# Last weight columns copied within DRAM during the scan, and the first closing loads moved into the unit in front

## The chip, the cores and the metric

The kernel runs on one NeuronCore of a Trainium2 chip. The metric is the device time of one execution in microseconds: the median of several runs. A separate execution was profiled; every row below comes from it. The engines are TensorE (PE, with its weight loads as PEld), VectorE (DVE), ScalarE (ACT), GpSimd (POOL) and SyncE (SP), which computes nothing and issues nearly all DMAs. POOL issues the DMAs that add into DRAM.

## The reference, cut to what matters

One decoder layer on 1024 tokens with 2048 channels, in float32, and a closing norm:

```python
hn = rmsnorm(h, norm_gain)
proj = hn @ w_in                       # pool input | pool gate | SSM input | SSM gate
ya = pool_mixer(pool_in, w_pool, pool_scale) * silu(pool_gate)
yb = ssm_mixer(ssm_in, ..., w_glu) * silu(ssm_gate)    # a complex-diagonal scan, then GELU and GLU
h = h + concatenate([ya, yb]) @ w_out
h = h + (p @ w_ple) * sigmoid(h @ w_ple_gate)
return rmsnorm(h, final_gain)
```

The change touches the last product, `h @ w_ple_gate`, in its last 512 of 2048 output columns, and what is loaded for it.

## The kernel before

Every float32 operand of a large product is split into a high and a low part that PE can multiply at full rate: ACT casts the high part (L213, L203, L401, L1415, L1430), DVE subtracts to get the low part (all on the helper line L102), and three matmuls (high-high, high-low, low-high) replace one. The program is a hand-written list of `steps`, each with its matmuls, a list `pre` of what is issued in front of them and `post` of what follows. `emit(s)` goes through them in order; it also splits the weights of the next steps and issues loads of the next weight chunks (buffers `raw`, three of them) ahead of time. Nothing reorders the instructions afterwards: each engine and SP's queue work in the order in which they are written. An instruction that waits holds up all that stands behind it on its engine.

The stretches that matter here:

- **Input projection and scan.** Blocks of `hn @ w_in` (L257) fill PE. Beside them a generator issues the state-space work piece by piece. One piece of it (`ss_v`) loads pairs `vb` and `vu` (sixteen groups, 0 to 15, each 256 KB and 256 KB) and multiplies them on PE (L881) into `aux`, in between the projection's matmuls.
- **Fourteen units.** Eight for `w_out`, six for the first 1536 columns of `w_ple_gate`; each unit forms the seven products of a Strassen-like scheme in fourteen steps (L235). The operands are 28 slots of a pool of 32 (`s_p`), called `cb`; a product's four slots are used for the last time in the last unit of a half, and come free there product by product. A step's result is added by DVE to `zs`; where it is the last part, ACT takes the sigmoid, DVE multiplies by `ze`, and POOL adds the tile into `z_d` in DRAM (L1323). Later steps go on adding into a bank whose intermediate value was read before.
- **Closing blocks.** The last 512 columns are done by token blocks (`tb` 0 to 7, 128 tokens each), four steps of twelve matmuls a block (L247), with the weights `wl` resident (16 tiles, one for each 128 rows) and the rows of `h` as the stationary side. In front of a step PE turns a tile `zn` (or the rows of `h` for the group g = 3) by four transposes into `bk` (L1454); the turned rows are normed and written out.

For block 0 all this must be there when the last unit (first step `s_l`) ends: the sixteen `wl` tiles, loaded by `wl_load` into the three `raw` buffers and split by `wl_split` into slots (L1409, L1415), four tiles of `h` (`h_load`, `h_split`, L1423, L1430), the tiles `zn`, and `fg`, the closing gain broadcast to all partitions (L1400, L1404).

Of the kernel before, what the change touches and what calls it, by code (L numbers as in the profile page):

```python
# [8 lines left out]
F32 = mybir.dt.float32  # L9
# [3 lines left out]
ALU = mybir.AluOpType  # L13
# [3 lines left out]
P = 128  # L17
L = 1024
HT = 512
D = 2048  # L20
# [19 lines left out]
def hybrid_trunk(ctx: ExitStack, tc: tile.TileContext, x, p, norm_gain, w_in, w_pool, pool_scale,  # L40
# [3 lines left out]
    sp = nc.sync  # L44
    dve = nc.vector
    act = nc.scalar
# [4 lines left out]
    p = p[0, 0]  # L51
    out = out[0]
# [5 lines left out]
    w_ple_gate = w_ple_gate[0].rearrange("(k p) c -> p k c", p=P)  # L58
# [4 lines left out]
    r_p = ctx.enter_context(tc.tile_pool(name="r_p", bufs=3))  # L63
# [16 lines left out]
    e_d = dr.tile([3 * HT, L], F32, name="e_d")  # L80
    en_d = dr.tile([L, HT], F32, name="en_d")
    ps_d = dr.tile([3 * HT, L], F32, name="ps_d")
    z_d = dr.tile([3 * HT, L], F32, name="z_d")
    gq_d = dr.tile([W, L], F32, name="gq_d")
    B_d = dr.tile([P, G, P], F32, name="B_d")
# [3 lines left out]
    def st(dt=F32, shape=(P, HT), name="st"):  # L89
        return st_p.tile(list(shape), dt, tag="st", name=name)  # L90

    def slot(name):
        return s_p.tile([P, 2, HT], F32R, tag="S", name=name)
# [4 lines left out]
    def f(ap):  # L98
        return ap.bitcast(F32)

    def tt(eng, o, a, b, op):
        eng.tensor_tensor(out=o, in0=a, in1=b, op=op)  # L102
# [1009 lines left out]
    def in_block(mb, halves=(0, 1)):  # L1112
        block(in_cols(mb), ALLK, halves, hn_key, ("pi", mb), v_post(mb))
        if 1 in halves:
            steps[-1]["post"].append(lambda: bg.append(pool_win(mb // 2, mb % 2)))
# [10 lines left out]
    in_block(6)  # L1126
    in_block(7)
    i_g = len(steps)
    in_block(4)
    pool_mm(3)  # L1130
    in_block(5)
# [273 lines left out]
                         in_=final_gain[L + i * GW:L + (i + 1) * GW].partition_broadcast(P))  # L1405

    def wl_load(k):
        fin["wl", k] = r_p.tile([P, 4, P], F32, tag="raw", name="raw").rearrange("p a c -> p (a c)")
        sp.dma_start(out=fin["wl", k], in_=w_ple_gate[:, k, 3 * GW:])  # L1409

    def wl_split(k):
        raw = fin.pop(("wl", k))
        sl = slot("wl")
        acts["wl", k] = sl[:, 0], sl[:, 1]
        act.copy(out=sl[:, 0], in_=raw)  # L1415
        tt(dve, sl[:, 1], raw, f(sl[:, 0]), ALU.subtract)

    def rows4(src, g, tb):
        return src[4 * g * P:4 * (g + 1) * P, tok(tb)].rearrange("(k q) t -> q k t", q=P)
# [11 lines left out]
        tt(dve, sl[:, 1], f(sl[:, 1]), f(sl[:, 0]), ALU.subtract)  # L1431

    def zn_load(tb, g):
        fin["z", tb, g] = st(name="zn")
        sp.dma_start(out=fin["z", tb, g].rearrange("p (k t) -> p k t", k=4),
                     in_=rows4(xT_d if g == 3 else z_d, g, tb))

# [78 lines left out]
                                     (lambda i=part.start // 256: last_part(i)))  # L1516
    s_l = units[-1][1]
    for k in range(KD):
        at = s_l + 2 + 3 * k // 4
        steps[at]["pre"].append(lambda k=k: wl_load(k))  # L1520
        steps[at + 2]["pre"].append(lambda k=k: wl_split(k))
    steps[i_t[0] - 2]["pre"].append(fg_load)
    for tb in range(NB):
        for g in range(4):
            at = s_l + 10 + g if tb == 0 else i_t[0] + g - 2 if tb == 1 else i_t[tb - 2] + g
            steps[at]["pre"].append(lambda tb=tb, g=g: h_load(tb, g))
            at = max(at + 3, i_t[tb - 1] + g) if tb else s_l + 13
            steps[at]["pre"].append(lambda tb=tb, g=g: h_split(tb, g))
            if tb == 0:
                at = i_t[0] + {3: 1, 0: 2, 1: 3, 2: 4}[g]  # L1530
            else:
                at = i_t[tb] + g + (tb == 1)
                if (tb, g) == (1, 3):
                    at -= 1
            steps[at - 3]["pre"].append(lambda tb=tb, g=g: zn_load(tb, g))
            steps[at]["pre"].append(lambda tb=tb, g=g: z_turn(tb, g))
        steps[i_t[tb]]["pre"].append(lambda tb=tb: en_load(tb))
        if tb < NB - 1:
            steps[i_t[tb + 1] + 2]["pre"].append(lambda tb=tb: final(tb))
# [70 lines left out]
```

## Time and profile before

| | |
|---|---|
| median of the runs | 1704.83 us (1703.92 to 1708.3) |
| the profiled execution | 1705.38 us, of which the span of instructions 1703.3 us |
| PE busy | 97% of the span |
| DVE, ACT, POOL busy | 66%, 42%, 9% |
| mean DMA rate | 198 GB/s |

The span is what the profiler saw from the first to the last instruction; the profiled execution has another 2.1 us around it. Busy shares are averages over stages with different limits. A row of a timeline gives start, length, engine, line, operation, tiles, count, and in brackets the idle time of the engine in front of it with what ended it. SPq rows are SP issuing a DMA: the time is that of the issue, not of the transfer. The granted clock of PE is a share of 2.4 GHz.

### The profile page before, as it was taken

What the parts mean: (1) busy time and instruction counts of PE and PEld (TensorE: products, weight loads), DVE (VectorE), ACT (ScalarE), POOL (GpSimd) and SP (SyncE); (2) the same over time, 40 slices, a digit from 0 to 9 for tenths busy, and PEclk for the clock granted to TensorE, in tenths of its full rate; (3) what the DMA queues carried; (4) which work ended last, traced back from release to release, by engine and by line L of the source; (5) the groups of instructions that cost most, each with busy time, mean ns of one, the idle gap of its engine ahead of it and who ended that gap; (6) DMA issues with size and microseconds to landing.
All of it is one profiled execution on the core that took longest, in us unless ns stands there. A gap on an engine that the chain in (4) does not pass through costs nothing.

```text
span 1703.3 us, 22940 instructions
## 1 busy us (share of the span) xinstructions
PE 1655.8 (97%) x7622; PEld 1369.0 (80%) x7622; DVE 1115.7 (66%) x2148; ACT 718.2 (42%) x1511; POOL 160.2 (9%) x267
## 2 busy tenths in 40 slices
PE   8999999999999999999999999999998899999797
PEld 7888887888888888888778877888886788787686
DVE  5763699468786645656646787658456756877554
ACT  6652255352113642333643354336333534434453
POOL 0067000000000210000000001111111100021000
PEclk9999999999999999999999999999999899999899
DMA  8872444462233753667955668868679957888995
GB/s 260 251 191 73 117 133 135 155 186 75 68 118 117 230 173 103 193 194 240 328 210 173 210 250 244 229 167 241 159 194 275 302 208 277 273 212 212 298 268 159
DMA packets 332104, 336.41 MB, mean 198 GB/s; under 512 B 56025, under 2 KB 225010, under 8 KB 330994
## 3 DMA queue, kind: packets, MB, share of 16 engines
q1 hardware_dynamic: 319314, 311.88, 57.1%
q0 software_dynamic: 12672, 23.07, 8.6%
q8 instruction: 60, 0.98, 0.2%
q14 instruction: 58, 0.48, 0.1%
HBM read 222.15 MB, written 119.01 MB: 200 GB/s over the span
## 4 chain that ended last, share of the span: by engine, by line
PE 47%; DMA 6%; DVE 3%; issue 2%; ACT 1%; SPq 0%; ACTq 0%; POOLq 0%; POOL 0%; DVEq 0%
PE mm L235 23%; PE aux L235 9%; PE mm L257 9%; PE mm L247 5%; DMA cb<-cm_d 1%; DMA cm_d<-cq 1%; DMA raw<-in_w_ple_gate_dram 1%; PE bk L1454 1%; DVE cb L102 1%; DMA e_d<-et 1%; DMA cb<-ya_d 1%; DMA zn<-xT_d 1%; DVE w L102 1%; DVE zs L102 0%; DMA cb<-xT_d 0%
## 5 line engine op out<-in xcount | busy, mean ns | idle before, releaser
L257 PE MATMUL mm<-hn,w 128*128 128x512 f32 x3072 | 722.2, 393 | 1.8 <-DVE w L102 1.2
L257 PEld LDWEIGHTS mm<-hn,w 128*128 128x128 f32 x3072 | 572.2, 188 | 119.7 <-DVE w L102 1.7
L235 PE MATMUL mm<-cb,w 128*128 128x512 f32 x2160 | 500.8, 391 | 8.6 <-ACT w L203 3.1
L235 PEld LDWEIGHTS mm<-cb,w 128*128 128x128 f32 x2160 | 405.4, 188 | 98.2 <-DVE w L102 5.1
L213 ACT CAST w<-raw 128x256 fp32r<-128x256 f32 x324 | 128.2, 407 | 279.4 <-PE mm L257 219.1
L102 DVE TENSOR_TENSOR w<-raw,w 128x256 fp32r<-128x256 f32 (+1 forms) x328 | 141.0, 441 | 121.4 <-ACT w L213 113.3
L102 DVE TENSOR_TENSOR w<-wq,w 128x512 fp32r<-128x512 f32 x216 | 148.3, 686 | 104.0 <-ACT w L203 103.7
L235 PE MATMUL aux<-cb,w 128*128 128x512 f32 x864 | 205.5, 393 | 7.7 <-ACT w L203 7.7
L235 PEld LDWEIGHTS aux<-cb,w 128*128 128x128 f32 x864 | 163.0, 189 | 44.4 <-ACT w L203 9.3
L203 ACT CAST w<-wq 128x512 fp32r<-128x512 f32 x216 | 133.6, 620 | 134.3 <-PE mm L235 54.8
L1286 POOL DMA_DIRECT2D xT_d<-ot x64 | 55.4, 866 | 670.3 <-DVE ot L102 634.7
L102 DVE TENSOR_TENSOR cb<-cb 128x512 fp32r<-128x512 f32 x140 | 91.6, 685 | 32.8 <-ACT cb L401 32.3
L247 PE MATMUL mm<-wl,h 128*128 128x512 f32 (+1 forms) x432 | 100.9, 386 | 5.7 <-ACT h L1430 5.7
L401 ACT CAST cb<-cb 128x512 fp32r<-128x512 f32 x140 | 82.3, 621 | 40.8 <-DMA cb<-xT_d 13.7
L247 PEld LDWEIGHTS mm<-wl,h 128*128 128x128 f32 x432 | 75.7, 196 | 19.2 <-ACT h L1430 6.1
L102 POOL TENSOR_TENSOR ytm<-yt,mask 128x512 f32<-128x512 f32 x16 | 20.0, 1250 | 441.5 <-DMA yl<-L_d 310.7
L1292 ACT COPY ot<-mm 128x512 f32<-128x512 f32 x48 | 28.2, 587 | 75.7 <-PE mm L235 73.3
L102 DVE TENSOR_TENSOR wq<-wq 128x1024 f32<-128x1024 f32 x36 | 43.8, 1217 | 0.0
L499 ACT ACTIVATE gs<-mm 128x512 f32<-128x512 f32 x32 | 18.9, 598 | 58.3 <-DVE mm L102 57.0
L1323 POOL DMA_DIRECT2D z_d<-zs x24 | 20.7, 863 | 230.0 <-DVE zs L102 230.0
L891 DVE COPY V<-aux 64x128 f32<-64x128 f32 x64 | 24.6, 384 | 25.2 <-ACT V L893 24.8
L102 DVE TENSOR_TENSOR w<-t,w 128x512 fp32r<-128x512 f32 x36 | 24.5, 685 | 19.2 <-ACT w L203 19.2
(209 smaller groups left out, 1558.1 us busy)
## 6 DMA issues: line engine op xcount, KB each, us to landing
raw<-in_w_in_dram SPq DMA_DIRECT2D x136, 256.0 KB, 2.9
cb<-cm_d SPq DMA_DIRECT2D x80, 256.0 KB, 5.2
wq<-in_w_out_dram SPq DMA_DIRECT2D x16, 1024.0 KB, 9.0
xT_d<-ot POOLq DMA_DIRECT2D x64, 256.0 KB, 6.4
cm_d<-cq SPq DMA_DIRECT2D x48, 256.0 KB, 3.9
wq<-in_w_ple_gate_dram SPq DMA_DIRECT2D x12, 1024.0 KB, 9.1
xT_d<-xt SPq DMA_DIRECT2D x32, 256.0 KB, 4.2
wq<-in_w_glu_dram SPq DMA_DIRECT2D x16, 512.0 KB, 6.9
```

What stands on the lines that cost most here:

```text
L102: eng.tensor_tensor(out=o, in0=a, in1=b, op=op)
L203: act.copy(out=w[0], in_=src)
L213: act.copy(out=w[:, 0], in_=raw)
L235: pe.matmul(out=banks[key], lhsT=w[wi][:, kp], rhs=a[:, ai], start=bool(new) and n == 0, stop=n == 11, skip_group_check=True)
L247: pe.matmul(out=banks[key][:, part], lhsT=a[:, ai, cols], rhs=b[:, part], start=start and j == 0, stop=stop and j == 2)
L257: pe.matmul(out=banks[key], lhsT=w[:, wi, i], rhs=a[:, ai], start=start and i == 0 and j == 0, stop=stop and i == 1 and j == 2)
L401: act.copy(out=sl[:, 0], in_=f(sl[:, 1]))
L499: act.activation(out=s, in_=b, func=AF.Sigmoid)
L891: dve.tensor_copy(out=o.rearrange("p k c -> p c k"), in_=i)
L1286: pool.dma_start(out=pair(xT_d, 4 * cg + 2 * c + b, h), in_=t, accum_op=ALU.add)
L1292: act.copy(out=t, in_=banks[name, k, b])
L1323: pool.dma_start(out=pair(z_d, mb, h), in_=t, accum_op=ALU.add)
```

## The change

The sixteen tiles of the last 512 columns of `w_ple_gate` are first copied within DRAM into a new tensor `wl_d`, by sixteen DMAs on SP's queue, one every two steps from 120 steps before `i_g` (`i_wl`). In the last unit `wl_load` reads `wl_d` straight into the low half of a slot, and `wl_split` makes both halves in place. Loads of `wl` start two steps later than before and go two to a step, each split three steps after its load. `fg` is loaded eight steps before the last unit, the four `h` tiles of block 0 in steps 2 and 3 of the last unit (before: 10 to 13), their splits in steps 6 to 9 (before: all in 13). Three of block 0's four tiles to be turned use the `raw` buffers and are loaded in steps 8, 10 and 12. `h_load` of block 1 moves one step later. Arithmetic and the matmuls are the same.

```diff
+    wl_d = dr.tile([D, HT], F32, name="wl_d")
...
     i_g = len(steps)
+    i_wl = i_g - 120
...
     def wl_load(k):
-        fin["wl", k] = r_p.tile([P, 4, P], F32, tag="raw", name="raw").rearrange("p a c -> p (a c)")
-        sp.dma_start(out=fin["wl", k], in_=w_ple_gate[:, k, 3 * GW:])
+        fin["wl", k] = slot("wl")
+        sp.dma_start(out=f(fin["wl", k][:, 1]), in_=wl_d[k * P:(k + 1) * P])

     def wl_split(k):
-        raw = fin.pop(("wl", k))
-        sl = slot("wl")
+        sl = fin.pop(("wl", k))
         acts["wl", k] = sl[:, 0], sl[:, 1]
-        act.copy(out=sl[:, 0], in_=raw)
-        tt(dve, sl[:, 1], raw, f(sl[:, 0]), ALU.subtract)
+        act.copy(out=sl[:, 0], in_=f(sl[:, 1]))
+        tt(dve, sl[:, 1], f(sl[:, 1]), f(sl[:, 0]), ALU.subtract)
...
     def zn_load(tb, g):
-        fin["z", tb, g] = st(name="zn")
+        if tb == 0 and g != 2:
+            fin["z", tb, g] = r_p.tile([P, 4, P], F32, tag="raw", name="raw").rearrange(
+                "p a c -> p (a c)")
+        else:
+            fin["z", tb, g] = st(name="zn")
...
     for k in range(KD):
-        at = s_l + 2 + 3 * k // 4
+        at = s_l + 4 + 2 * (k // 4) + k % 4 // 2
         steps[at]["pre"].append(lambda k=k: wl_load(k))
-        steps[at + 2]["pre"].append(lambda k=k: wl_split(k))
-    steps[i_t[0] - 2]["pre"].append(fg_load)
+        steps[at + 3]["pre"].append(lambda k=k: wl_split(k))
+        steps[i_wl + 2 * k]["pre"].append(lambda k=k: sp.dma_start(
+            out=wl_d[k * P:(k + 1) * P], in_=w_ple_gate[:, k, 3 * GW:]))
+    steps[s_l - 8]["pre"].append(fg_load)
     for tb in range(NB):
         for g in range(4):
-            at = s_l + 10 + g if tb == 0 else i_t[0] + g - 2 if tb == 1 else i_t[tb - 2] + g
+            at = s_l + 2 + g // 2 if tb == 0 else i_t[0] + g - 1 if tb == 1 else i_t[tb - 2] + g
             steps[at]["pre"].append(lambda tb=tb, g=g: h_load(tb, g))
-            at = max(at + 3, i_t[tb - 1] + g) if tb else s_l + 13
+            at = max(at + 3, i_t[tb - 1] + g) if tb else s_l + 6 + g
...
-            steps[at - 3]["pre"].append(lambda tb=tb, g=g: zn_load(tb, g))
+            if tb == 0 and g != 2:
+                steps[s_l + 8 + 2 * ((g + 1) % 4)]["pre"].append(lambda g=g: zn_load(0, g))
+            else:
+                steps[at - 3]["pre"].append(lambda tb=tb, g=g: zn_load(tb, g))
```

What it moves on the engines, at three places. The first is SP's queue in the stretch with `ss_v`: `raw` are weight chunks of `w_in`, `vb` and `vu` the loads of one group for PE, `sg_d` a store. Before:

```order
L193 DMA raw<-in_w_in_dram 128x4x128
L185 DMA sg_d<-gs 128x512 x2
L868 DMA vb<-B_d 128x512
L856 DMA vu<-u_d 128x4x128
L868 DMA vb<-B_d 128x512
L856 DMA vu<-u_d 128x4x128
L193 DMA raw<-in_w_in_dram 128x4x128
```

And now:

```order
L194 DMA raw<-in_w_in_dram 128x4x128
L186 DMA sg_d<-gs 128x512 x2
L1527 DMA wl_d<-in_w_ple_gate_dram 128x512
L869 DMA vb<-B_d 128x512
L857 DMA vu<-u_d 128x4x128
L869 DMA vb<-B_d 128x512
L857 DMA vu<-u_d 128x4x128
L194 DMA raw<-in_w_in_dram 128x4x128
L1527 DMA wl_d<-in_w_ple_gate_dram 128x512
```

A copy now stands in front of each two pairs of `vb` and `vu`; eight of the sixteen copies stand so, six ahead of them among stores, two behind.

The second is SP's queue in the second half of the last unit and behind it: `raw` from `w_ple_gate` and `wl` are the last columns, `zs` and `ze` what the unit's own results need, `zn` (or `raw` from `xT_d` and `z_d`) what is turned. Before:

```order
L1409 DMA raw<-in_w_ple_gate_dram 128x512
L1423 DMA h<-xT_d 128x4x128
L1315 DMA ze<-e_d 128x512
L1409 DMA raw<-in_w_ple_gate_dram 128x512 x2
L1423 DMA h<-xT_d 128x4x128
L1409 DMA raw<-in_w_ple_gate_dram 128x512
L1400 DMA fg<-in_final_gain_dram 128x1024
L1404 DMA fg<-in_final_gain_dram 128x512 x2
L1423 DMA h<-xT_d 128x4x128
L1435 DMA zn<-xT_d 128x4x128
L1423 DMA h<-xT_d 128x4x128
L1409 DMA raw<-in_w_ple_gate_dram 128x512
```

And now, from the last pairs of `wl` on:

```order
L1411 DMA wl<-wl_d 128x512 x2
L1440 DMA raw<-z_d 128x4x128
L1317 DMA ze<-e_d 128x512
L1411 DMA wl<-wl_d 128x512 x2
L1440 DMA raw<-z_d 128x4x128
L1424 DMA h<-xT_d 128x4x128
L1445 DMA en<-en_d 128x512
L1424 DMA h<-xT_d 128x4x128 x2
L1440 DMA zn<-z_d 128x4x128
```

The four `h` of block 0 and `fg` are no longer here; the `h` rows that are left belong to block 1, and the only `zn` of block 0 that is still loaded behind the unit is that of group 2.

The third is DVE in steps 8 to 10 of the last unit: `w` is the split of weights for a step two ahead, the two `zs` rows are add and multiply of a result. Before:

```order
L102 TENSOR_TENSOR w<-wq,w 128x512
L102 TENSOR_TENSOR wl<-raw,wl 128x512
L102 TENSOR_TENSOR zs<-mm,zs 128x512
L102 TENSOR_TENSOR zs<-zs,ze 128x512
L102 TENSOR_TENSOR w<-wq,w 128x512
L102 TENSOR_TENSOR wl<-raw,wl 128x512
```

And now:

```order
L103 TENSOR_TENSOR w<-wq,w 128x512
L103 TENSOR_TENSOR wl<-wl 128x512 x2
L103 TENSOR_TENSOR h<-h 128x512
L103 TENSOR_TENSOR zs<-mm,zs 128x512
L103 TENSOR_TENSOR zs<-zs,ze 128x512
L103 TENSOR_TENSOR w<-wq,w 128x512
L103 TENSOR_TENSOR wl<-wl 128x512 x2
```

Between two results stand now two splits of `wl` in every step, and one of `h` in four steps, where one or two of `wl` stood and the four of `h` came together near the end.

## Rows read from the trace of the kernel before

**Rows 1.** PE's timeline, last two gate units to block 1: start, length, instructions.

```profile
1499.07 16.48 PE L235 MATMUL mm<-cb,w 128*128 128x512 f32 x72
...
1537.15 16.48 PE L235 MATMUL mm<-cb,w 128*128 128x512 f32 x72
...
1565.55 3.00 PE L235 MATMUL mm<-cb,w 128*128 128x512 f32 x12 [1.04 <-DVE zs L102]
...
1571.59 5.60 PE L235 MATMUL aux<-cb,w 128*128 128x512 f32 x24
1582.87 4.89 PE L247 MATMUL mm<-wl,h 128*128 128x512 f32 x12 [5.68 <-ACT h L1430]
1591.36 1.12 PE L1454 MATMUL bk<-ident,zn 128*128 128x128 f32 x4 [3.60 <-DMA zn<-xT_d]
...
1600.85 3.02 PE L247 MATMUL mm<-wl,h 128*128 128x512 f32 x12
...
1604.06 3.00 PE L247 MATMUL mm<-wl,h 128*128 128x512 f32 x12
```

**Rows 2.** Stretches: length, busy time of each engine, granted clock, DMA share, GB/s.

```profile
1580.20:1586.80 6.60, 3.93 (x9) 3.03 (x10) 3.28 (x5) 2.28 (x4) 0.86 (x1) 0.50 1.03 265
```

**Rows 3.** SP's waits, 1480 to 1620: total us, times, longest.

```profile
SPq L1409 <- DVE wl L102: 18.7, 9, 8.2
```

**Rows 4.** SP's timeline: issues in the unit in front and behind the last.

```profile
1504.72 2.36 SPq L1315 DMA_DIRECT2D ze<-e_d  x2
...
1580.89 1.02 SPq L1423 DMA_DIRECT2D h<-xT_d  x1
```

**Rows 5.** DVE's timeline in the last gate unit.

```profile
1549.20 0.68 DVE L102 TENSOR_TENSOR zs<-mm,zs 128x512 f32<-128x512 f32 x1
...
1551.19 0.68 DVE L102 TENSOR_TENSOR w<-t,w 128x512 fp32r<-128x512 f32 x1
1551.79 1.29 DVE L102 TENSOR_TENSOR wl<-raw,wl 128x512 fp32r<-128x512 f32 x2
```

**Rows 6.** DMA issues from 1537 to 1604: count, size, median us to landing.

```profile
z_d<-zs POOLq DMA_DIRECT2D x10, 256.0 KB, 6.9
...
zn<-z_d SPq DMA_DIRECT2D x6, 256.0 KB, 6.0
```

**Rows 7.** The chain that ended last, near block 0: start, length.

```profile
1582.02 9.30 DMA zn<-xT_d
```

**Rows 8.** SP's timeline: issues of vu for groups 6, 8 and 14.

```profile
344.40 0.47 SPq L856 DMA_DIRECT2D vu<-u_d  x1
...
350.13 0.38 SPq L856 DMA_DIRECT2D vu<-u_d  x1
...
373.72 0.44 SPq L856 DMA_DIRECT2D vu<-u_d  x1
```

**Rows 9.** PE's timeline: groups 6, 8, 13 and 14.

```profile
349.86 1.05 PE L881 MATMUL aux<-vu,vb 128*128 128x128 f32 x8
...
357.14 1.05 PE L881 MATMUL aux<-vu,vb 128*128 128x128 f32 x8
...
375.28 1.05 PE L881 MATMUL aux<-vu,vb 128*128 128x128 f32 x8
...
379.16 1.13 PE L881 MATMUL aux<-vu,vb 128*128 128x128 f32 x8
```

**Rows 10.** The tile vu: its loads, issue to landing.

```profile
DMA to landing us min/median/max: 3.3/4.9/5.4
```

**Rows 11.** DMA issues of the whole span: count, size, median us to landing.

```profile
raw<-in_w_in_dram SPq DMA_DIRECT2D x136, 256.0 KB, 2.9
...
z_d<-xT_d SPq DMA_DIRECT2D x3, 10.0
```

**Rows 12.** Stretches, columns as in rows 2.

```profile
300.00:400.00 100.00, 99.90 (x505) 84.70 (x504) 57.17 (x129) 43.36 (x107) 0.00 (x0) 1.00 0.49 151
1537.00:1604.00 67.00, 56.49 (x233) 45.07 (x232) 43.32 (x66) 26.48 (x49) 8.62 (x10) 0.90 0.94 244
```

## The prediction

> **What bounds the kernel now.** I first read the busy shares on the page: PE has work in nearly the whole span, so a microsecond can only be won where PE idles or runs slowly. I then looked in PE's timeline for rows with idle time in front of them. The largest group stands where the last gate unit (fourteen steps, numbered 0 to 13 here) hands over to the closing blocks. Step 0 starts at 1537.15 and a step takes 2.72 us (72 matmuls are six steps). Step 10 waits 1.04 us, step 13 ends at 1577.2, the first closing matmul waits 5.68 us for the split of h, the first turn waits 3.60 us for zn, and the twelve matmuls between these waits need 4.89 us for work that later takes 3.00 [rows 1]. The granted clock says why: 0.50, the lower of the two levels (1.2 GHz), from 1580.2 to 1586.8, the stretch in which PE had stopped [rows 2]. From 1604.06, where block 1 begins, PE has no further gap until its matmuls end.
>
> Third, why the data is late. SP issues nearly every DMA, in program order. Its waits show 18.7 us spent on the release of raw by the splits of wl, so it reaches the third load of h only at 1580.89 [rows 3, 4]. Fourth, why DVE is slow to release them: from 1549.20 on it is a queue of back-to-back work. One gated result (add, wait for ACT's sigmoid, multiply) takes 1.99 us (1549.20 to 1551.19), a split of w 0.60 (1551.19 to 1551.79), and each other operation on 512 columns the same, so two splits of wl 1.20 [rows 5].
>
> **The change part by part, in the last unit and behind it.** The number of splits is the same; the raw buffer, and with it SP's wait for DVE, is gone. h is loaded in steps 2 and 3, wl from step 4, two a step. A wl now needs a free slot when it is loaded, so SP waits for PE instead (the first products give four slots back after step 1, four after step 3, and so on). Behind that wait stand the ps and e loads of the running unit; PE frees slots two to three steps before those loads are used, so I cost it at nothing. If that cover were gone, each late one would add its landing to DVE's queue.
>
> I follow DVE by hand, in the new order, because it becomes the busiest engine of the unit: 1.99 + 0.60 + 1.20 (+ 0.60 with an h) is 3.8 to 4.4 us a step against PE's 2.72. It is level with PE until the result of step 6, done at about 1557.1. Step 7 (w, two wl, h, one add of 0.60) ends at 1560.1. Step 8: 2.4 of splits to 1562.5, gate to 1564.5. Step 9: to 1566.9 and 1568.9. Step 10, without h: 1570.7 and 1572.7. Step 11: 1574.5 and 1576.5. Step 12, without w: 1577.7 and 1579.7. Step 13: 1580.9 and 1582.9; the last two wl at 1584.1. PE feels it twice: step 11 adds into the bank that the result of step 9 is read from (read by 1567.6, due 1567.1, with the start about 0.7 lost), and step 13 needs its w (1573.4, due 1573.2). So step 13 ends at about 1576.3, 0.9 earlier than now.
>
> Then nothing is missing for the first closing steps: h and wl 0 to 3 are split by 1566, zn of group 3 has been loaded since about step 8, PE does not idle and keeps the upper clock. A closing step with its turn takes 3.21 us (1600.85 to 1604.06) [rows 1]; the fourth starts at 1585.9 and its wl are ready at 1584.1. Block 1 could begin at 1576.3 + 4 x 3.21 = 1589.1 instead of 1604.06: **15.0 us** is the most that this end can give.
>
> **What is late next.** The turn of group 2 stands right in front of block 1, and its load waits for the additions into z_d from step 11. That result is ready at 1576.5; from its issue the addition takes 6.9 us in this stretch, the load of zn behind it 6.0 [rows 6]: 1576.5 + 6.9 + 6.0 = 1589.4, against 1588.7 needed (1589.1 less the turn), and with two hand-overs in between about 1.0 us. SP stands at that wait until some 1583.6, and behind it are h of block 2 and zn of block 1, due from 1592; I add 1.0 us for the first of those. So 15.0 - 2.0 = **13.0 us**. Bounds: no wait at all when the loads are spread thinner, or 6.4 us when both take 9.3, like the zn at 1582.02 [rows 7] (1576.5 + 18.6 = 1595.1).
>
> fg moves to step 6 of the unit in front, between two e loads. SP issues those from 1504.72 on [rows 4]; PE, whose unit starts at 1499.07 [rows 1], is in step 6 at 1515.4. It costs three issues and 1 MB there and takes as much off the crowded end; the e behind it is multiplied after step 8, at 1523.6, some 16 us later. Nothing, then; if that lead were gone, fg's own landing. zn in raw buffers instead of st: nothing, since those buffers are idle once wl leaves them.
>
> **The part with a price: sixteen copies.** They stand on SP's queue in front of pool work, one every two steps, eight of them right before loads of vb and vu. PE's aux matmuls take those in order, so a late pair stops PE. Now: a vu lands 4.9 us after its issue (5.4 at worst). Group 6 is issued at 344.40, lands at 349.3 to 349.8 and is used at 349.86: 0.1 to 0.6 us of slack, say 0.3. Group 14 is issued at 373.72 and PE starts it at 379.16, 0.25 us behind its pace (375.28 + 3.64; the two groups from 349.86 to 357.14 take 7.28): slack 0. Group 8 is issued at 350.13 and used at 357.14: 1.6 to 2.1 [rows 8 to 10]; every other group has about as much or more, read the same way. A copy delays what is behind it on SP and in the DMA engines by D. No row shows this copy. Nearest: a copy within DRAM of 2 MB lands after 10.0 us [rows 11]; an eighth of the bytes is 1.25 us. With an issue of 0.4 us, D = 1.6: group 6 loses 1.3, group 14 1.6, group 8 nothing: **2.9 us**. Bounds for D: 0.4 (the issue alone; the engines are only 49% busy from 300 to 400 [rows 12]), costing 0.1 + 0.4 = 0.5 us; and 3.4 (the whole landing of a 256 KB load of w_in, 2.9 [rows 11], and the issue, as if nothing overlapped), costing 3.1 + 3.4 + about 1.5 for group 8 and the like for one more: about 9.5. I take the copy's row because it is the only one that reads and writes DRAM. A gain is excluded: nothing is removed there.
>
> The Trainium skill (DMA: Bandwidth & Descriptors, Bandwidth) gives about 358 GB/s as what a core gets from HBM. A copy reads and writes there, so 2 x 262 KB would take 1.46 us, an estimate from that page, instead of 1.25; by it D is 1.9, the scan costs 3.5 and the sum comes out 0.6 us later. No run here has shown such a copy of 256 KB.
>
> **The sum.** The profiled execution took 1705.4 us (span 1703.3 and 2.1 around it); minus 13.0, plus 2.9, is 1695.3. It lies 0.55 above the median of the runs, so I forecast **1694.7 us**.
>
> **The rivals.**
> A. The copies hide fully and zn is in time. For it: DMA is half busy in that stretch, and PE waits only at group 14 now. Against: two groups without slack. 1705.4 - 15.0 = 1690.4, on the median's scale 1689.8.
> B. The wait only moves. DMA is busy 94% of 1537 to 1604 [rows 12], and in the first half of it some of the idle time is SP's waiting; what is loaded earlier collides with the additions into z_d, which are then slow. Price: the 6.4 us above, and the copies: 1705.4 - 15.0 + 6.4 + 2.9 = 1699.7, on the median's scale 1699.1. Against: fg has left that stretch, and the wl loads are issued before most of the additions.
> The Trainium skill (DMA: Bandwidth & Descriptors, Issuing engines are not separate DMA queues) says that all DMAs run on the same 16 engines and interleave; by that rule the earlier loads take time from the additions, as in B. The 94% agrees.
> C. Slower: the copies hold the vb and vu loads in the pool of DMA engines. From D of about 4 to 5 the three groups named and the five with about 2 us of slack lose more than the 13.0 of the end; at D = 5.5 groups 6, 14 and 8 lose 5.2 + 5.5 + 3.6 = 14.3 and the others up to 3.6 each, say 7 together: 1705.4 - 13.0 + 21.3 = 1713.7, 1713.1 on the median's scale. For it: that is about half of what a 2 MB copy takes, and a copy with rows of 2 KB may be cut worse than a whole one. Against: loads with such rows land in 2.9 us.
> D. The change does not do what it says, because DVE and not the loads holds the end: my own walk has DVE 3.8 to 4.4 us a step. If its lag reached PE in every step from 8 on (six steps of 1.4 us, less the 2.7 of slack), step 13 would end 5.7 late, 4.6 more than in my walk (1.1): 1705.4 - 13.0 + 4.6 + 2.9 = 1699.9, 1699.3 on the median's scale. Against: at every step the walk has what PE needs within 0.7 us.
>
> **How the numbers follow.** Forecast 0.58 (1692 to 1697.5), A 0.14, B 0.12, D 0.08, C 0.08. A measurement of this kernel can tell 0.3%, 5.1 us, from no change. The forecast and A are faster (0.72), B and D mostly (0.09 of 0.20), C is slower: faster 0.81, same 0.11, slower 0.08. The range goes from A with most of the walk's 1.1 us gone as well, 1689.0, to B and D with the upper part of the copies' price, 1702.0; what is left out is C and little else.
>
> **What would show it.** In the changed profile PE should have no idle row of 5 us between step 13 and block 1 and no granted clock of 0.50 there; the first closing matmul should follow the gate unit at once, and the only wait should be a turn for zn of group 2, of 0 to 3 us. DVE's splits of wl should come in pairs with no idle time for DMA before them. From 320 to 385 PE should wait for vu, at groups 6 and 14 only, by 1 to 2 us each; waits there at most groups mean C. Gaps in the gate unit's steps 8 to 13 that end on DVE mean D. A wait of over 5 us for zn means B. It would prove me wrong altogether if the closing stretch were as long as now although the loads are earlier.

## The result and the profile after

The changed kernel takes 1693.46 us (median; 1691.47 to 1698.0), the kernel before 1704.38 beside it: ratio 0.9937, interval 0.9919 to 0.9956. The forecast was 1694.7 in a range of 1689 to 1702. The profiled execution took 1694.17 us, 11.2 us less than that of the kernel before; its span is 1692.4 us, 10.9 us shorter.

PE's timeline of the changed kernel, last gate unit to block 1 (start, length, instructions, idle time in front), answers [rows 1]:

```profile
1541.53 16.48 PE L236 MATMUL mm<-cb,w 128*128 128x512 f32 x72
...
1572.24 2.97 PE L236 MATMUL mm<-cb,w 128*128 128x512 f32 x12 [0.63 <-DVE zs L103]
1575.05 5.60 PE L236 MATMUL aux<-cb,w 128*128 128x512 f32 x24
1580.49 2.89 PE L248 MATMUL mm<-wl,h 128*128 128x512 f32 x12
1583.21 0.60 PE L1459 MATMUL bk<-ident,raw 128*128 128x128 f32 x4
...
1592.82 0.60 PE L1459 MATMUL bk<-ident,zn 128*128 128x128 f32 x4
1593.18 3.00 PE L248 MATMUL mm<-wl,h 128*128 128x512 f32 x12
```

One wait of 0.63 us is left in this stretch. The closing matmuls follow the gate unit at once, no turn waits, and from step 0 to block 1 it is 1593.18 - 1541.53 = 51.65 us, where the kernel before needs 1604.06 - 1537.15 = 66.91 [rows 1]: **15.26 us gained**. The clock stays up; the stretches (busy time of PE, PEld, DVE, ACT, POOL, then granted clock, DMA share, GB/s) answer [rows 2, 12]:

```profile
1541.00:1593.00 52.00, 51.37 (x234) 42.18 (x233) 42.50 (x66) 25.08 (x47) 8.63 (x10) 1.00 1.01 280
300.00:400.00 100.00, 95.05 (x481) 80.11 (x480) 52.65 (x120) 41.73 (x104) 0.00 (x0) 1.00 0.64 183
1576.00:1586.00 10.00, 10.00 (x48) 8.26 (x47) 8.01 (x13) 5.44 (x10) 2.59 (x3) 1.00 0.78 172
```

But step 0 starts 4.38 us later than before, and 15.26 - 4.38 = 10.9 is what the span lost. Most of the delay arises in the scan. PE's timeline there, groups 0, 6 and 14, answers [rows 9]:

```profile
328.14 1.13 PE L882 MATMUL aux<-vu,vb 128*128 128x128 f32 x8 [1.21 <-DMA vu<-u_d]
...
352.46 1.13 PE L882 MATMUL aux<-vu,vb 128*128 128x128 f32 x8 [2.29 <-DMA vu<-u_d]
...
383.17 1.13 PE L882 MATMUL aux<-vu,vb 128*128 128x128 f32 x8 [1.45 <-DMA vu<-u_d]
```

Together 4.95 us, where the kernel before only starts group 14 0.25 us behind its pace. SP's queue shows what now stands in front of such a pair (here group 6 and the one behind it), and the tile vu how long its loads take (least, median, most), as [rows 8, 10]:

```profile
343.97 0.50 SPq L1527 DMA_DIRECT2D wl_d<-in_w_ple_gate_dram  x1
344.51 0.60 SPq L869 DMA_DIRECT2D vb<-B_d  x1
345.21 0.41 SPq L857 DMA_DIRECT2D vu<-u_d  x1
```

```profile
DMA to landing us min/median/max: 4.8/5.8/6.7
```

So a copy costs its issue, 0.50 us, and by the medians over all groups 0.9 more until a vu has landed (4.9 before). At group 14 it is 1.0 more: 6.3 us from issue to landing instead of 5.3.

SP's waits from 1480 to 1620 (total us, times, longest) answer [rows 3]. The 18.7 us at the release of raw are gone; wl now waits for PE's slots, and one long wait has come, in front of the zn of group 2:

```profile
SPq L1440 <- DMA z_d<-zs: 6.9, 1, 6.9
...
SPq L1411 <- PE mm L236: 3.9, 5, 1.6
```

### The profile page after: what moved, and what is told of

It reads as the page before. It is cut to its first block, busy times and chain, and to the rows that moved or that the text cites. A ratio compares the mean times of both kernels' runs of the same rounds, so it can differ in the third digit from the quotient of the medians.

```text
span 1692.4 us, 22974 instructions
## 1 busy us (share of the span) xinstructions
PE 1650.8 (98%) x7622; PEld 1364.9 (81%) x7622; DVE 1116.8 (66%) x2148; ACT 716.7 (42%) x1511; POOL 160.2 (9%) x267
## 4 chain that ended last, share of the span: by engine, by line
PE 49%; DMA 4%; DVE 3%; issue 2%; ACT 1%; SPq 0%; ACTq 0%; POOLq 0%; POOL 0%; DVEq 0%
PE mm L236 24%; PE aux L236 10%; PE mm L258 8%; PE mm L248 5%; DMA cb<-cm_d 1%; DVE cb L103 1%; PE bk L1459 1%; DVE w L103 1%; DMA cb<-ya_d 1%; DMA wq<-in_w_ple_gate_dram 1%; DMA e_d<-et 1%; DMA cb<-xT_d 0%; DMA wl<-wl_d 0%; DVE zs L103 0%; DMA zs<-ps_d 0%
## 5 line engine op out<-in xcount | busy, mean ns | idle before, releaser
L248 PE MATMUL mm<-wl,h 128*128 128x512 f32 (+1 forms) x432 | 96.5, 374 | 0.0
L894 ACT COPY V<-aux 64x128 f32<-64x128 f32 x64 | 24.4, 381 | 31.1 <-DVE V L892 22.4
```

Of the source, the lines that this page charges most:

```text
L248: pe.matmul(out=banks[key][:, part], lhsT=a[:, ai, cols], rhs=b[:, part], start=start and j == 0, stop=stop and j == 2)
L894: act.copy(out=o.rearrange("p k c -> p c k"), in_=i)
```

## Experiments

Behind block 1 all kernels are alike (99.2 to 99.6 us to the end of the span). So each is told by three numbers of its profile: the waits of aux for vu (for the kernel before, the lateness of group 14), the start of step 0 of the last unit, and the time from there to block 1. What lies ahead of step 0 differs by 1 to 3 us from profile to profile of kernels that are alike there, so the second number is coarser than the third.

| kernel | waits in the scan | step 0 at | to block 1 | median us | ratio, interval |
|---|---|---|---|---|---|
| before | 0.25 | 1537.15 | 66.91 | 1704.38 | |
| changed | 4.95 | 1541.53 | 51.65 | 1693.46 | 0.9937, 0.9919 to 0.9956 |
| changed_again | 3.74 | 1540.16 | 51.69 | 1694.76 | 0.9938, 0.9925 to 0.995 |
| copies_alone | 3.75 | 1541.11 | 66.43 | 1709.19 | 1.0024, 1.0014 to 1.0034 |
| copies_later | 0.1 | 1538.52 | 51.66 | 1688.62 | 0.9906, 0.9892 to 0.9919 |
| copies_behind | 0 | 1536.12 | 51.65 | 1688.74 | 0.9905, 0.9888 to 0.9921 |
| copies_on_act | 3.01 | 1541.85 | 51.66 | 1694.99 | 0.9944, 0.9932 to 0.9957 |
| copies_behind_twice | 6.05 | 1546.67 | 51.62 | 1699.61 | 0.9968, 0.9957 to 0.9979 |
| h_fg_only | 0 | 1539.93 | 61.61 | 1701.05 | 0.9977, 0.9967 to 0.9987 |
| wl_only | 4.16 | 1543.90 | 56.64 | 1701.67 | 0.9976, 0.9967 to 0.9984 |
| no_copies | 0.3 | 1538.70 | 57.26 | 1697.32 | 0.9958, 0.9941 to 0.9974 |
| zn_crowded | 6.21 | 1545.28 | 51.64 | 1696.07 | 0.9946, 0.9933 to 0.996 |
| zn_late | 3.76 | 1542.62 | 51.64 | 1691.02 | 0.993, 0.9916 to 0.9944 |
| later_and_zn_late | 0.2 | 1537.85 | 51.66 | 1690.57 | 0.9924, 0.9904 to 0.9944 |

In some of these profiles one of the three waits is put down to DVE (V or w) instead of vu. It stands at the same group, and in copies_alone the vu loads around group 14 land 6.7 to 7.1 us after their issue, so I count it with the others; that is a reading, not a row.

Part of what blurs the second number lies ahead of the scan: h_fg_only does nothing differently before the unit in front of the last, yet reaches group 0 at 331.03, 2.93 us later than the kernel before, and step 0 2.78 later. The price of the copies is read more closely from the start of group 0 to that of group 15. The kernel before:

```profile
328.10 1.05 PE L881 MATMUL aux<-vu,vb 128*128 128x128 f32 x8
...
382.88 1.05 PE L881 MATMUL aux<-vu,vb 128*128 128x128 f32 x8
```

These are 54.78 us, and 54.5 to 55.0 in the five others that have no copy there, or have them between the pairs (copies_later, copies_behind, h_fg_only, no_copies, later_and_zn_late). The changed kernel and copies_alone need 58.77 and 58.66, so 3.9 to 4.0 more; copies_on_act needs 57.98. In changed_again, wl_only, zn_late and zn_crowded it is 60.3 to 61.0, 5.5 to 6.3 more: besides the waits, the granted clock falls behind one of them, from 2.4 GHz to 1.2 for a part of the next 5 us. PE's timeline of changed_again, and the stretch behind its wait at group 14:

```profile
383.33 1.13 PE L882 MATMUL aux<-vu,vb 128*128 128x128 f32 x8 [1.88 <-DMA vu<-u_d]
384.21 4.58 PE L258 MATMUL mm<-hn,w 128*128 128x512 f32 x12
```

```profile
383.40:388.60 5.20, 5.20 (x20) 4.32 (x21) 2.37 (x6) 1.91 (x5) 0.00 (x0) 0.67 0.21 68
```

The twelve matmuls take 4.58 us where they take 3.0 elsewhere. In the changed kernel's first profile the clock stays at 1.00 behind a longer wait (2.29 us); what decides it is open.

### What the copies cost, and why

**The copies alone,** in the kernel before:

```diff
+    wl_d = dr.tile([D, HT], F32, name="wl_d")
+    i_wl = i_g - 120
+        steps[i_wl + 2 * k]["pre"].append(lambda k=k: sp.dma_start(
+            out=wl_d[k * P:(k + 1) * P], in_=w_ple_gate[:, k, 3 * GW:]))
```

> The kernel before, with the sixteen copies into wl_d added at the steps where the changed kernel has them; nothing reads them, and nothing else is changed (extra work, nothing left out). Theory T (the copies only cost, because they stand in SP's queue in front of vb and vu pairs that have no slack): waits of aux for vu at groups 0, 6 and 14, together 4.5 to 5 us where the kernel before has 0.25, the end as before; 1704.4 + 4.6 = about 1709, ratio 1.0025 to 1.003. Rival R1 (the waits in the changed kernel have another cause, such as a different run of the clock or of the splits): no such waits, 1704.4, ratio 1.000.

Measured 1709.19 against 1706.07 for the kernel before in these rounds: 3.1 us more by the medians, 4.1 by the ratio of 1.0024. That is T, with 3.75 us of waits instead of 4.5 to 5. PE's timeline has the waits of groups 6 and 14 (none at group 0), and an end as long as ever:

```profile
351.76 1.13 PE L882 MATMUL aux<-vu,vb 128*128 128x128 f32 x8 [1.83 <-DMA vu<-u_d]
...
382.97 1.13 PE L882 MATMUL aux<-vu,vb 128*128 128x128 f32 x8 [1.92 <-DVE V L892]
...
1586.54 4.80 PE L248 MATMUL mm<-wl,h 128*128 128x512 f32 x12 [6.15 <-ACT h L1432]
```

**The copies 32 steps later,** in the changed kernel:

```diff
-    i_wl = i_g - 120
+    i_wl = i_g - 88
```

> The changed kernel with the copies 32 steps later, behind the loads of vb and vu (about 385 to 475 us), where the DMA engines are a quarter busy and no pair is waited for. Theory T: the waits at groups 0, 6 and 14 go back to the 0.25 us of the kernel before, the end is unchanged, 1693.5 - 4.7 = about 1689, ratio 0.991. Rival R2 (a copy costs some time of PE wherever it stands, since it takes DMA engines from whatever runs): other loads are waited for instead, 3 to 5 us between 385 and 480, and about 1693, ratio 0.9935.

T again: 1688.62, no wait of 0.5 us or more between 300 and 500 us, and PE busy throughout:

```profile
300.00:400.00 100.00, 99.94 (x505) 84.79 (x504) 56.85 (x130) 45.08 (x111) 0.00 (x0) 1.00 0.51 155
400.00:500.00 100.00, 100.00 (x442) 82.79 (x442) 83.31 (x291) 18.86 (x45) 1.30 (x1) 1.00 0.46 132
```

**The copies between the two pairs,** one step later:

```diff
-        steps[i_wl + 2 * k]["pre"].append(lambda k=k: sp.dma_start(
+        steps[i_wl + 2 * k + 1]["pre"].append(lambda k=k: sp.dma_start(
```

> The changed kernel with each copy one step later, so that it stands between the two pairs of vb and vu that it stood in front of: as many copies in the same stretch, another place in the queue. Theory T (the place in the queue sets the delay of what stands right behind it): the waits at groups 0, 6 and 14, whose pairs now stand in front of their copy, fall from 4.95 to under 1.5 us together; odd groups have 2 us or more to spare and wait by under 1 us together; about 1690.5. Rival R3 (the copies are sheer load on the DMA engines, whatever stands in front): waits of 4 to 5 us stay, 1693 to 1694.

1688.74, and no wait at all, better than T had it. Sheer load (R3) is refuted as the cause at this size: the DMA engines carry as much from 300 to 400 us as in the changed kernel (share 0.65 against 0.64), yet PE works without a gap:

```profile
300.00:400.00 100.00, 100.00 (x506) 84.82 (x505) 57.75 (x130) 44.02 (x109) 0.00 (x0) 1.00 0.65 194
```

**The copies on ACT's queue:**

```diff
-        steps[i_wl + 2 * k]["pre"].append(lambda k=k: sp.dma_start(
+        steps[i_wl + 2 * k]["pre"].append(lambda k=k: act.dma_start(
```

> The changed kernel with the sixteen copies issued by ACT at the same steps instead of SP: the same bytes at about the same time, but nothing on SP's queue. Theory T: of the delay of the vb and vu loads the part that is SP's issue (0.5 us for each copy, 1.0 for group 0 with two in front) is gone at least, and if the rest is order in the queue that goes too: waits at groups 0, 6 and 14 between 0.5 and 3 us together instead of 4.95, 1689 to 1691.5, unless ACT's own 0.5 us for each issue delays a cast of w. Rival R3 (sheer load on the DMA engines): 4 to 5 us of waits stay, 1693 to 1694.

3.01 us of waits remain and the time, 1694.99, is that of the changed kernel; T's 1689 to 1691.5 missed, R3 is nearer. One load tells how. SP's and ACT's issues at group 14, and the landing of this vu:

```profile
374.34 0.45 SPq L857 DMA_DIRECT2D vu<-u_d  x1
374.40 0.50 ACTq L1527 DMA_DIRECT2D wl_d<-in_w_ple_gate_dram  x1
```

```profile
DMA to landing us min/median/max: 7.2/7.2/7.2
```

The vu was issued 0.06 us ahead of the copy and lands after 7.2 us. In copies_behind the copy follows 0.5 us after the same vu, on SP's own queue, and that vu lands after 5.0:

```profile
373.28 0.46 SPq L857 DMA_DIRECT2D vu<-u_d  x1
373.78 0.56 SPq L1527 DMA_DIRECT2D wl_d<-in_w_ple_gate_dram  x1
...
DMA to landing us min/median/max: 5.0/5.0/5.0
```

In the kernel before it was 5.3, in the changed kernel, behind the copy, 6.3. So on one queue the copy delayed what stood behind it and not what stood in front, and from ACT's queue it took time from a load that was already under way. This rests on one load and on group 6, which fits: PE starts it 6.91 us after the issue of its vu, ACT's copy following 0.07 us behind, where copies_behind has 5.58. Where ACT's copy came 1.0 and 1.4 us behind the vu (groups 8 and 10), the vu landed after 5.0 and 5.1 us, against 4.1 and 4.7 in copies_behind. Whether the other queue or the shorter distance (0.06 us against 0.5) makes most of the difference was not separated. The Trainium skill (DMA: Bandwidth & Descriptors, Queues, rings and completion order) says that each DMA engine takes the descriptors of one ring in order and goes round between the rings of different issuers; the rows of group 14 agree. The same page (Rules for kernel authors) says that spreading DMAs over issuers only saves issue time; here it saved 0.5 us of SP and the load in flight took about 2 us longer.

**Every copy twice, between the pairs:**

```diff
+        steps[i_wl + 2 * k + 1]["pre"].append(lambda k=k: sp.dma_start(
+            out=xx_d[k * P:(k + 1) * P], in_=w_ple_gate[:, k, 3 * GW:]))
```

> The version with each copy between the two pairs of vb and vu, with every copy made twice, the second into a tensor that nothing reads: 32 copies, all behind the even pairs (extra work, nothing left out). Theory Q (on one queue a transfer doesn't slow what was issued in front of it; what counts is what stands in front): the vu of groups 6 and 14 land in 5.0 to 5.6 us as with single copies and those groups still don't wait; the odd groups, with two copies in front, lose up to 2 us at one or two places; 1689 to 1692. Rival R3 (sheer load): with twice the load vu lands 6 to 7 us after its issue in every group, waits of 4 to 8 us at groups 6 and 14 and others, 1693 to 1698.

Both theories missed the time: 1699.61. PE's timeline has waits at groups 0 and 7, and the first wait brings the clock down (twelve matmuls in 4.39 us instead of 3.0):

```profile
332.48 2.05 PE L883 MATMUL aux<-vu,vb 128*128 128x128 f32 x8 [4.77 <-DMA vu<-u_d]
334.18 4.39 PE L259 MATMUL mm<-hn,w 128*128 128x512 f32 x12
...
361.63 1.13 PE L883 MATMUL aux<-vu,vb 128*128 128x128 f32 x8 [1.28 <-DMA vu<-u_d]
```

Group 7 has two copies in front of it, as Q says (its vu lands after 7.4 us). Groups 6 and 14 start without a wait 5.15 and 5.47 us after the issue of their vu (351.42 to 356.57, 381.64 to 387.11), so those landed as fast as with single copies: R3's waits there aren't seen. What Q left out is group 0, in front of whose pair stand the copies of two steps, now four: 4.77 us and another 2.3 for the clock. And the load isn't nothing at this size: group 8, with no copy within 3 us in front of it, lands after 6.6.

**The changed kernel again:**

> The changed kernel once more, beside the others on one chip, so that the versions with other places of the copies (1688.7) can be held against it: 1693.5, with waits for vu of 4 to 5 us from 320 to 385 us. If the places of the copies made no difference and the chips did, it is at 1689 here.

1694.76 (1692.84 to 1698.05), on the chip of copies_later and copies_behind; waits of 1.86 and 1.88 us at groups 6 and 14 and none at group 0. Copies_later (1687.59 to 1691.19) and copies_behind (1685.21 to 1691.04) are 6 us below it. The places of the copies account for most of that: 3.74 us of waits and the 1.6 of the lower clock behind the second.

### Which part wins the end

**h and fg moved alone,** in the kernel before:

```diff
-    steps[i_t[0] - 2]["pre"].append(fg_load)
+    steps[s_l - 8]["pre"].append(fg_load)
-            at = s_l + 10 + g if tb == 0 else ...
+            at = s_l + 2 + g // 2 if tb == 0 else ...
-            at = max(at + 3, i_t[tb - 1] + g) if tb else s_l + 13
+            at = max(at + 3, i_t[tb - 1] + g) if tb else s_l + 6 + g
```

> The kernel before with two parts of the change alone: the loads and splits of h of block 0 and the load of fg stand where the changed kernel has them. No copies, wl still through the three raw buffers, zn as before. Its end can be compared with 15.3 us, what the changed kernel wins from step 0 of the last unit to block 1, and its time with 1704.4 - 15.3 = 1689. Theory T (SP standing at the release of raw is what makes the end late): SP still waits 10 us or more for raw, so zn and the last wl stay late; PE idles 4 to 8 us between step 13 and block 1, and the time is 1693 to 1697. Rival H (it was the place of h and fg in the queue): no idle row over 1 us there, 1689 to 1690.5, and the copies and the slots are for nothing.

The end gains 66.91 - 61.61 = 5.3 us, and the time is 1701.05: T's mechanism, but T's time was too low by 4. It forgot the lower clock behind the waits: the end is 9.96 us longer than the changed kernel's, of which 6.7 are idle time and 3.3 slower matmuls. SP still stands 19.1 us at raw, and reaches zn at 1583.91 after 6.84 us for three loads of raw. Timelines of SP and PE, and SP's waits:

```profile
1577.02 6.84 SPq L1409 DMA_DIRECT2D raw<-in_w_ple_gate_dram  x3
1583.91 0.45 SPq L1435 DMA_DIRECT2D zn<-xT_d  x1
```

```profile
1569.67 7.16 PE L235 MATMUL mm<-cb,w 128*128 128x512 f32 x24 [2.30 <-DVE zs L102]
...
1589.99 1.12 PE L1454 MATMUL bk<-ident,zn 128*128 128x128 f32 x4 [5.00 <-DMA zn<-xT_d]
```

```profile
SPq L1409 <- DVE wl L102: 19.1, 10, 5.5
```

**wl alone:** the changed kernel with the three lines on h and fg put back.

> The changed kernel with h of block 0 and fg back at the places of the kernel before (h loaded in steps 10 to 13, split in 13, fg in the last steps); copies, wl through slots and early zn stay. Theory T (SP standing at the release of raw makes the end late): SP reaches those h about 10 us earlier than before, PE idles 2 to 5 us in front of the first closing matmul because the last splits of h stand behind DVE's queue, and the time is 1693.5 + 2 to 5 = 1695.5 to 1698.5. Rival H (the place of h and fg): idle 5 us or more with the granted clock at 0.50 behind it, 1701 or more. The median landing of the additions into z_d, 6.2 to 7.0 us so far, says too whether fg and h crowd them.

66.91 - 56.64 = 10.3 us of the end, and 1701.67. PE's first closing matmul waits for h, split behind DVE's other work, and then runs at the lower clock:

```profile
1586.12 4.63 PE L248 MATMUL mm<-wl,h 128*128 128x512 f32 x12 [3.98 <-ACT h L1431]
```

The idle time is T's (2 to 5 us), the total is H's number but not by H's cause. The end is 56.64 - 51.65 = 5.0 us longer than the changed kernel's, 3.4 of it idle time and 1.6 the lower clock; on changed_again's 1694.76 that gives 1699.8. From group 0 to group 15 the two need the same 60.3 us, so the other 2 us are not the scan's; the profile has them between the scan and step 0, and what they are is open. The additions into z_d land in 6.6 us (median), so h and fg don't crowd them. In the profiles the parts of the end add up: 5.3 + 10.3 = 15.6 against 15.26 together, two thirds of it wl with the early zn, one third h and fg, so neither T nor H alone. The medians don't add up as well: 4.2 us for h and fg and 3.6 for wl, which pays for the copies, against 10.5 for the changed kernel in the same rounds.

**No copies, more buffers:** h_fg_only with

```diff
-        fin["wl", k] = r_p.tile([P, 4, P], F32, tag="raw", name="raw").rearrange("p a c -> p (a c)")
+        fin["wl", k] = st(name="wr") if k % 2 else r_p.tile(
+            [P, 4, P], F32, tag="raw", name="raw").rearrange("p a c -> p (a c)")
-        at = s_l + 2 + 3 * k // 4
+        at = s_l + 4 + 2 * (k // 4) + k % 4 // 2
```

> The kernel before with h and fg moved as in h_fg_only, and with the wl loads two a step as in the changed kernel, but from the weights themselves: even tiles into the three raw buffers, odd ones into st, so that about twice as many buffers stand between SP and DVE's splits. No copies and no wl_d. Theory T (what the end needs is SP not standing at DVE's release; the copy only makes loading in place possible): SP's wait for raw falls from 19 to under 8 us, 52 to 57 us from step 0 of the last unit to block 1 where h_fg_only has 61.6, and 1689 to 1694. Rival K (loads from the contiguous copy are what brings wl in time): SP still stands over 12 us at raw or st and the end takes 59 us or more, 1698 or more.

57.26 us and 1697.32: between the two. Twice the buffers, with the loads two a step, win 61.61 - 57.26 = 4.35 of the 10 us that h_fg_only still lacks. SP still waits 6.1 us for wl's splits at these loads and 3.6 at the ze behind them:

```profile
SPq L1410 <- DVE wl L102: 6.1, 2, 5.0
SPq L1315 <- DVE wl L102: 3.6, 2, 2.3
```

Loads from the weights land in 5.1 and 5.7 us (median), those from wl_d in 5.5: the copy doesn't make the load quicker. What it does is let a tile be loaded where it stays. Whether loading in place needs the copy isn't shown: a kernel that loads the slots straight from `w_ple_gate` wasn't tried.

### The term that vanished: zn of group 2

**Four more copies in front of that zn,** in the changed kernel:

```diff
+    for k in range(4):
+        steps[i_t[0] + 1]["pre"].append(lambda k=k: sp.dma_start(
+            out=xx_d[k * P:(k + 1) * P], in_=w_ple_gate[:, k, 3 * GW:]))
```

> The changed kernel with four more copies of 256 KB within DRAM, into a tensor that nothing reads, issued by SP directly in front of the load of zn of group 2 (extra work, nothing left out). Theory Z (in the changed kernel the last addition into z_d landed in 3.7 us, not 6.9, because SP, standing 6.9 us at the wait for it, had issued nothing and the DMA engines had run empty): with 1 MB more in the engines the addition takes 6 to 7 us and zn behind it 5 to 6, so the turn of group 2 waits about 1 to 3 us, 1694.5 to 1696.5. Rival Z2 (additions issued by POOL are served beside SP's transfers at their own pace): it lands in about 4 us as before, no wait, 1693.5.

Z's mechanism, not its price. SP's timeline, then the landing of the last addition that zn waits for (issued at 1585.13 here), and that of zn:

```profile
1582.04 2.56 SPq L1525 DMA_DIRECT2D xx_d<-in_w_ple_gate_dram  x4
1591.67 0.37 SPq L1441 DMA_DIRECT2D zn<-z_d  x1
```

```profile
DMA to landing us min/median/max: 6.4/6.4/6.4
...
DMA to landing us min/median/max: 3.2/3.2/3.2
```

The addition takes 6.4 us; in the changed kernel it took 3.7. The zn behind it then finds the engines nearly idle (share 0.28 from 1591.7 to 1593), lands in 3.2, and is in time for the turn at 1596.57. The 1.3 us in the median over changed_again isn't told from nothing; the end takes 51.64 us here too.

**zn as before:** the changed kernel with the two places `if tb == 0 and g != 2` made `if False`.

> The changed kernel with one part undone: the three tiles zn of block 0 that it loads early into the raw buffers (groups 3, 0 and 1) are loaded into st three steps ahead of their turn, as in the kernel before. Theory T (zn was late before only because SP was): SP reaches them at about 1574 to 1576 on the scale of the changed kernel, they land by about 1583 and are needed from 1583.2 on, 3.2 us apart; at most 1 us of waiting, 51.7 to 52.7 us from step 0 of the last unit to block 1, 1694 to 1695. Rival Z3 (the early zn is a part that the end needs): the first turn waits 3 to 5 us as before, 55 to 57 us, 1697 to 1699.

51.64 us and no wait: T's mechanism. The early zn in raw buffers wins nothing. The addition takes 6.4 us here as well, beside the later loads of zn, and its turn doesn't wait either. The time, 1691.02, is 3 us below T's, though the copies stand where they cost: three of the five executions took 1690.7 to 1691.0 us, two 1695.3 and 1695.9. The profile is of the one with 1695.3; what the three faster ones did differently no profile shows.

**The two together:**

> Both edits that looked better than the changed kernel or equal to it: the copies 32 steps later, and zn of block 0 loaded three steps ahead of its turn. No waits for vu, 51.6 to 51.7 us from step 0 of the last unit to block 1, and 1687 to 1689.5. If the two parts disturb each other (which no row so far shows), 1690 or more.

51.66 us and 1690.57, just above its range; the rows show no disturbance, and its interval overlaps those of copies_later and copies_behind. It differs from zn_late only in the place of the copies and ran on the same chip (another than that of copies_later), yet the two medians, 1690.57 and 1691.02, are equal within noise. So the 6 us between the copies' places are measured with the early zn on one chip, and were not found again with the late one on another; the profiles of the two (0.2 and 3.76 us of waits) differ as in the first pair. Copies_later and copies_behind are the best that was run: 1688.6 and 1688.7, with ranges below that of the changed kernel, and with nothing in the profile to choose between them.

## Why the prediction was right, point by point

**What bounds the kernel: right.** The row at half the clock and the waits of 5.68 and 3.60 us [rows 1, 2] are gone, and h_fg_only and wl_only show that both of their causes, SP at raw and the late h, had to go.

**DVE's walk: right within 0.2 us.** Shifted by the 4.38 us of step 0, it has the additions of steps 8, 9 and 11 at 1566.9, 1571.3 and 1578.9 and the last splits of wl done at 1588.5. The timeline of DVE says 1567.01, 1571.41, 1579.01 and 1588.7 (1587.39 + 1.29):

```profile
1567.01 0.69 DVE L103 TENSOR_TENSOR zs<-mm,zs 128x512 f32<-128x512 f32 x1
...
1571.41 0.68 DVE L103 TENSOR_TENSOR zs<-mm,zs 128x512 f32<-128x512 f32 x1
...
1579.01 0.69 DVE L103 TENSOR_TENSOR zs<-mm,zs 128x512 f32<-128x512 f32 x1
...
1587.39 1.29 DVE L103 TENSOR_TENSOR wl<-wl 128x512 fp32r<-128x512 f32 x2
```

PE's wait at step 11 was to be 0.7 and is 0.63. The 15.0 us that this end was to give at most are 15.26: rival D is out. It worked because every duration came from [rows 5] and the order was known.

**What is late next: wrong, 2.0 us too dear.** The failed step is "from its issue the addition takes 6.9 us in this stretch, the load of zn behind it 6.0". These are medians over 67 crowded microseconds [rows 6]; the addition came at their end, while SP stood 6.9 us at the wait for it and issued nothing. The window from 1576 to 1586 shows it (DMA share 0.78 and 172 GB/s, against 1.01 and 280 over the whole stretch), and its last 2 us more so:

```profile
1584.00:1586.00 2.00, 2.00 (x11) 1.60 (x10) 2.00 (x4) 0.59 (x2) 0.86 (x1) 1.00 0.25 46
```

POOL's timeline has the issue of the addition at 1581.38. It landed in 3.7 us (second row), and SP went on at 1585.25, in time:

```profile
1581.38 0.86 POOL L1325 DMA_DIRECT2D z_d<-zs  x1 [2.94 <-DVE zs L103]
...
DMA to landing us min/median/max: 3.7/3.7/3.7
```

Zn_crowded gives the 6.4 us back by filling the engines. It also shows that the two terms can't simply be added: with the addition at 6.4 the zn took 3.2 instead of 6.0, and nothing waited. Rival B fell for the same reason.

**The copies: the mechanism right, 1 to 2 us too cheap.** 2.9 us was the term. The waits of the first profile are 4.95 - 0.25 = 4.7 and of the second 3.7, copies_alone is 3.1 to 4.1 us longer, and from group 0 to group 15 the price is 3.9 to 4.0, or 5.5 and more where the clock falls behind a wait, which the term left out. D was right where I could see the slack: group 14 lost 1.45 and 1.88 for 1.6 (issue 0.5, landing 5.3 to 6.3). Group 6 lost 2.29 and 1.86 for 1.3. And group 0 lost 1.21 or nothing: "every other group has about as much or more" left out that two copies (issued at 319.82 and 321.00), not one, stand in front of its pair. Its vu landed 2.6 us later than before (328.04 against 325.43), nearly all of its 2.67 us of slack; so PE waits there only in a profile in which it comes early, as in the first (at 326.93, 1.2 us ahead of the kernel before), and not in changed_again. Why group 6 loses more than group 14 is open: its vu is issued 0.81 us later than before and used 7.25 us after that instead of 5.46, and the trace lacks its landing.

**The sum.** -13.0 + 2.9 was to be -10.1; it is -15.26 + 4.38 = -10.9. Two errors of 2.3 and 1.5 us have opposite signs, so that the sum is off by only 0.8 is in part luck. The rest of the 1.2 us under the forecast is the time around the span (1.8 us instead of 2.1) and the place of the profiled execution above the median (0.7 instead of 0.55). Rival A (1689.8) was wrong about the kernel that was made, since the copies didn't hide; with the copies moved, copies_later and copies_behind measure its 1689. Rival C's argument that loads with rows of 2 KB land in 2.9 us reads the wrong row: those tiles of w_in come as 128x4x128, in pieces of 512 bytes. C's price was far off all the same.

**fg and the waits for slots at nothing: right.** No new idle row stands in the unit in front, and SP's 3.9 us at PE's slots reach no engine.

## What to carry to other kernels

Before a transfer is put on a queue, look at the slack of what stands directly behind it, for each load and not on average: moving sixteen copies by one step won another 6 us on top of the change's 11, on one chip and with everything else as in the changed kernel. The duration of a transfer is to be taken from rows in the same company: here the engines were 0.25 busy at the end of a long wait of the issuing queue. A short wait of PE can cost more than its length, 1.6 us here, when the clock falls behind it. Where loads are late because their buffers wait for a slow engine, loading into the place where the tile stays takes that engine out of the queue.

## What the hardware showed

A copy of 256 KB within DRAM took 0.50 us to issue, and the seven whose landing the trace of the changed kernel has landed in 3.9 to 5.4 us. With a copy issued from ACT's queue 0.06 us after a load, that load took 7.2 us, where with the same copy 0.5 us behind it on SP's own queue it took 5.0: here the order within one queue protected the earlier transfer. Whether another queue at the same distance would have hurt it as much wasn't tried.
